# Top-k of query tiles 5 to 7 spread over attention, and attention in two passes over the heads

## Chip, cores and metric

The kernel runs on one core of a Trainium2 chip. The metric is device time in microseconds (us) of one execution; smaller is better. A core has five engines with a queue each, worked off in order: PE (TensorE, matrix products), DVE (VectorE), ACT (ScalarE), POOL (GpSimd) and SP (SyncE, which here only issues DMAs). PE writes into PSUM, and DVE and ACT evict from there into SBUF.

## What is computed

One layer of a streaming encoder, for 1024 new frames (query tiles 0 to 7 of 128 rows) and 32 frames of a running stream with 512 cached ones (tile 8). Sizes: D_MODEL 1024, 8 query heads on 4 key/value heads of 64, 8 indexer heads, 8 recurrent heads, hidden layer 4096.

```python
xn = rms_norm(x, norm_mix)
zq, zk, zv, ziq, zik, ziw, zs = split(xn @ w_in)
# group A: sparse attention
dots  = einsum('bthd,bsd->bths', qi, ki_all) * IDX_DIM ** -0.5
score = einsum('bths,bth->bts', relu(dots), wi)          # indexer
score = where(arange(L) < (qpos // 64 + 1) * 64, score, -inf)
_, idx = top_k(score, 256 or L // 4)
o_att = softmax attention of q over the chosen keys only
# group B: rwkv7, a matrix state carried along the frames
S = S * w_t - (S kk_t) b_t + v_t k_t ;  y_t = S r_t      # per head
h = x + concat(o_att, o_rwkv) @ w_out
y = h + square(relu(rms_norm(h, norm_ffn) @ w_ff1)) @ w_ff2
```

A query keeps its 256 best keys; for tiles 0 and 1 all admissible keys are kept, so the top-k runs for tiles 2 to 8. The kernel does not gather. It finds each row's threshold and adds a large negative mask to the attention scores of all other keys.

## The kernel before

A framework orders the instructions: each has a priority from its place in the traced program (and from high_priority blocks), and each engine's queue is filled with what is ready in a modelled timeline, by that priority. A tile of memory is given to the next user when all readers of the previous one are done. Generators in the program interleave the stages.

**Input projections** (phase_a). Keys and indexer keys of all tiles, then indexer queries and the scores S.sc[t] of tiles 2 to 8 (idx_tile), then K and Q of attention (norm_tile, 18 calls) and the recurrence's inputs (zs_block, 14 calls, whose matmuls are L440 and whose evictions on ACT are L449 and L450). Scores of tiles 4 to 8 lie in one tile G of 4096 columns, those of 2 and 3 in tiles named AR.

**Top-k** (topk, two generators in tk). The threshold is found bit by bit in 31 rounds. The first group, tiles 2, 3, 4 and 8, counts on DVE (L342); the second, tiles 5, 6 and 7, counts on ACT with the Sign function (L362), three operations and three accumulator reads a round. Three small DVE operations (L364, L365, L367) then set the next threshold, on which the next round waits. step(1) stands behind each norm_tile and each zs_block and takes one step of both generators; step(100) takes what is left of 32. masks() drains the rest: for the second group an exact correction (L342, L381, L382), then for both Sign, Square, a running count and the mask (L396, L397, L402, L403, L404). It works in S.eq, which is the tile KB of the pool te, and in junk tiles named AR.

**Recurrence** (rwkv_all). Five units of 256 frames (the last one of 32). Per unit: a front (lora products, decay sums L647, KB and AR by L681, products L712 masked by L715 into G, four transposes L824, a triangular inverse on POOL in L829 and L831, transposes L835 and L840), a join (L768 to L779), token transposes (L746 to L752) and four sequential steps per unit (L876 to L911), then a norm. Units 0, 2 and 4 use tiles KB, AR and G of the pool rp. Units 1 and 3 use KB of te and AR and G of S.tk, the very tiles of the top-k. The triangular inverse has one set of buffers for all units.

**Attention** (attn_all). Items are pairs of key/value head j and tile t, for j = 0 to 3 and t in ORD. At t = 8 and t = 0 prep transposes the head's keys (L1062, L1064, L1067, L1068) into K and Kl, which have one buffer. Per item: query (L1080 to L1087), scores for two heads (L1099, L1100, masked and reduced by L1102 on DVE, exponential L1105 on ACT, into one of three tiles s), then turn (transposes L1123, copies L1124 alternately on ACT and DVE) and product (L1139 with V, L1143 to L1146, stored by L1147). The next item's begin runs between the turns of the present one.

The program calls the recurrence eight steps ahead, then masks(), and then takes one step of ga (attention) and one of gr (recurrence) in turn. Output projection (project, L1256; tiles 0 to 2 by project_early, into tiles G, KB and AR of rp) and the MLP (L1320, L1340) follow.

Of the kernel before, what the change touches and what calls it, by code (L numbers as in the profile page):

```python
# [53 lines left out]
F32 = mybir.dt.float32  # L54
F32R = mybir.dt.float32r
BF16 = mybir.dt.bfloat16
# [10 lines left out]
NT = 9  # L67
# [83 lines left out]
def phase_a(S, pwx, pwy, pa, pi, px, xp, ps, late):  # L151
    nc, I, O = S.nc, S.I, S.O
# [73 lines left out]
    iw = pa.tile([128, NT, 8], F32, name="iw")  # L226

    G = S.tk.tile([128, 4096], F32, name="G")
    S.sc, c = {}, 0
    for t in range(4, NT):  # L230
        n = 664 if t == 8 else 128 * (t + 1)
        S.sc[t] = G[:, c:c + n]
        c += n
    for t in (2, 3):
        S.sc[t] = S.tk.tile([128, 128 * (t + 1)], F32, name="AR", bufs=4)
# [1 line left out]
    for SL in SLS:  # L237
        X = K()
# [4 lines left out]
        X.off = S.tk.tile([128, 2, len(SL)], F32, name="off" + str(len(SL)))  # L243
    ones = S.tk.tile([128, 1], F32, name="ones")
    nc.gpsimd.memset(ones, 1.0)
    junk, junk2 = [S.tk.tile([128, 1024], BF16, name="AR", bufs=4) for _ in range(2)]

    kiA = pi.tile([128, 1024], F32R, name="kiA")
    kiB = pi.tile([128, 1024], F32R, name="kiB")
# [95 lines left out]
    def topk(X):  # L345
# [9 lines left out]
        for i in range(30, -1, -1):  # L355
            if X.exact:
                count(X, ALU.is_lt, c_of, S.sc)
            else:
                for j, t in enumerate(X.SL):
                    r = rows_of(t)  # L360
                    n = S.sc[t].shape[1]
# [11 lines left out]
        if not X.exact:  # L373

            count(X, ALU.is_gt, c_of, S.sc)
            for j, t in enumerate(X.SL):
                r = rows_of(t)
                n = S.sc[t].shape[1]
                s = S.sc[t][:r, :n]
                e = S.eq[j % 2][:r, :n]  # L380
                nc.vector.tensor_scalar(e, s, c_of(j, r), BIG, op0=ALU.is_le, op1=ALU.mult)  # L381
                nc.vector.tensor_tensor_reduce(out=e, in0=e, in1=s, op0=ALU.add, op1=ALU.min, scale=1.0, scalar=FMAX,  # L382
                                               accum_out=cns[:r, j:j + 1])
                yield
            nc.vector.tensor_scalar(need, cnt, 256.0, None, op0=ALU.is_ge)
            nc.vector.tensor_tensor(cns, cns, cf, op=ALU.subtract)
            nc.vector.tensor_tensor(cns, cns, need, op=ALU.mult)
            nc.vector.tensor_tensor(cf, cns, cf, op=ALU.add)

        nc.vector.tensor_scalar(cns, cf, -1.0, None, op0=ALU.mult)  # L390
        for j, t in enumerate(X.SL):
            r = rows_of(t)
            g = S.sc[t][:r]
            a = [x[:r, j:j + 1] for x in (cnt, cns, need)]
            cum = S.eq[j % 2][:r, :g.shape[1]]
            nc.scalar.activation(g, g, AF.Sign, bias=a[1], accum_out=a[0])  # L396
            nc.scalar.activation(cum, g, AF.Square, accum_out=a[2])  # L397
            nc.vector.tensor_tensor(a[2], a[2], a[0], op=ALU.add)
            nc.vector.tensor_scalar(a[2], a[2], -0.5, 256.0, op0=ALU.mult, op1=ALU.add)
            n = keys_of(t)  # L400
            g, cum = g[:, :n], cum[:, :n]
            nc.vector.tensor_tensor_scan(cum, ones[:r].to_broadcast([r, n]), cum, 0.0, op0=ALU.add, op1=ALU.subtract)  # L402
            nc.vector.scalar_tensor_tensor(cum, cum, a[2], g, op0=ALU.is_gt, op1=ALU.is_gt)  # L403
            nc.scalar.activation(S.mb[t], cum, AF.Copy, scale=-BIG)  # L404
            yield
# [49 lines left out]
    tk = [topk(X) for X in TK]  # L455
# [43 lines left out]

    left = [32 - EARLY * (len(IDXO) - EI), 32]  # L500

    def step(n):
        for i, g in enumerate(tk):
            m = min(n, left[i])
            left[i] -= m
            for _ in range(m):
                next(g)
# [43 lines left out]
            yield  # L551

    def masks():
        for g in tk:
            for _ in g:
                pass
    return main, main2, main3, masks


# [484 lines left out]
def attn_all(S, ap, ps):  # L1044


    nc, I, O = S.nc, S.I, S.O
    items = [(j, t) for j in range(4) for t in ORD]
    J, W = {}, {}

    def prep(j, samp):
# [97 lines left out]

    def begin(k):  # L1150
        j, t = items[k]
        if t == 8 or t == 0:
            prep(j, t == 8)
        query(k)
        yield
        for h in range(2):
            scores(k, h)
            yield
        inverse_sums(k)
        yield  # L1160

    N = len(items)
    for _ in begin(0):
        yield
# [212 lines left out]
MA = 8  # L1377
# [8 lines left out]
RAT = 1  # L1386
XPB = 3
DINV = ()
ORD = [8,0,1,2,3,4,5,7,6]
ZQB = 3  # L1390
ACB = 2
HIM = 2
# [6 lines left out]
SLS = ((2,3,4,8),(5,6,7))  # L1399
IDXO = (2,3,4,5,8,6,7)  # L1400
PH = 4
AHEAD = 6
# [8 lines left out]
def body(tc, I, O, dbg=None):  # L1411
    nc = tc.nc
    S = K()
    S.nc, S.tc, S.I, S.O, S.dbg = nc, tc, I, O, dbg or {}
    pool = lambda **kw: tc.tile_pool(bufs=1, **kw)
    with pool(name="const") as cp, pool(name="dram", space=DRAM) as dp:
# [6 lines left out]
        def opened(name, side="left"):  # L1423
            p = pool(name=name, side=side)
            return p, p.__enter__()
# [5 lines left out]
        mp = S.mp  # L1431
        S.mb = {t: mp.tile([rows_of(t), keys_of(t)], BF16, name=f"mb{t}") for t in range(NT) if t != 7}
        S.xs = mp.tile([128, 8, 64], F32R, name="mb7")
        p1a, S.tk = opened("p1a", "right")
        with pool(name="xnt") as xp, pool(name="psA", space=PSUM) as ps:
            late = {}
# [3 lines left out]
            with pool(name="pi", side="right") as pi:  # L1440
                with pool(name="px", side="right") as px:
                    m1, m2, m3, masks = phase_a(S, pwx, pwy, pa, pi, px, xp, ps, late)
                    g = m1()
# [19 lines left out]
            with pool(name="pq") as pq:  # L1463
                g = m3(pq, 4, 7)
# [3 lines left out]
                gr = rwkv_all(S, RORD)  # L1468
# [17 lines left out]
        ga = attn_all(S, S.at, ps)  # L1486
        for _ in range(ATT0):
            next(ga)
        for i in range(EARLYF, max(AHEAD, MA)):
            if i == MA:  # L1490
                masks()
            next(gr)
        if MA >= AHEAD:
            masks()
        S.G.append(S.tk.tile([128, 2, 4, 4, 128], F32, name="G"))
        raw = wo = None
        gens = [ga, gr]
        while gens or wo is None:
            for g in list(gens):
                with (tc.high_priority(OFF) if g is gr else nullcontext()):  # L1500
# [37 lines left out]
```

## Time and profile before

| what | value |
|---|---|
| median of 3 timed runs | 1797.65 us (1793.79 to 1798.66) |
| profiled execution | 1798.12 us |
| its span, first to last instruction | 1796.3 us |
| mean granted clock of TensorE | 0.927 |
| busy in the span: PE, DVE, ACT, POOL | 93%, 52%, 39%, 34% |

The page gives busy time per engine, busy shares in 40 slices of 45 us (a digit is tenths, 9 is 90% or more), the chain of work that ended last, and the costliest groups of instructions by line. PEclk is the granted clock of TensorE, 1.00 being 2.4 GHz and 0.50 being 1.2 GHz. Groups read: out<-in, shapes, count | busy us, mean ns | idle time of the engine just before them and what ended it. In a stretch, "busy (x)" is the busy time and the number of records; accumulator reads count as records of their own.

### The profile page before, as it was taken

The numbers are of one execution on the slowest core, as the hardware profiler recorded it, in microseconds if no ns is written. First come the engines' busy times: TensorE is split into PE (matmuls) and PEld (weight loads), VectorE is DVE, ScalarE is ACT, GpSimd is POOL, SyncE is SP. The second block draws the span as 40 slices with busy tenths as digits, with TensorE's granted clock in tenths as the row PEclk, the third lists the DMA queues.
The fourth block names the chain that finished last, engine by engine and source line by source line (L and its number), as shares of the span: only waits on it lengthen the run. The fifth ranks groups of instructions, "written<-read, shape, count | busy, mean of one in ns | idle before, by whom it ended". The sixth has DMA issues, their size and how long they took to land.

```text
span 1796.3 us, 30013 instructions
## 1 busy us (share of the span) xinstructions
PE 1663.9 (93%) x11686; PEld 1509.2 (84%) x11686; DVE 936.1 (52%) x1996; ACT 707.6 (39%) x1549; POOL 618.6 (34%) x919
## 2 busy tenths in 40 slices
PE   7999979986569898999899999999999999999999
PEld 6787779986456777767678799999999999999998
DVE  6477889975878687577562533222222222222224
ACT  6365667897446344344641331222222121212120
POOL 7468863353543443056210021222222222222120
PEclk9999989996559697798899999999999999999999
DMA  7211131323110202140323341111111111111105
GB/s 218 54 36 43 42 88 64 110 68 92 29 27 14 40 24 57 26 101 17 98 76 123 121 125 49 46 48 45 49 37 53 42 53 42 47 44 51 36 16 172
DMA packets 180775, 113.25 MB, mean 63 GB/s; under 512 B 51969, under 2 KB 169817, under 8 KB 180633
## 3 DMA queue, kind: packets, MB, share of 16 engines
q1 hardware_dynamic: 171800, 107.00, 21.4%
q10 hardware_dynamic: 8832, 4.33, 0.9%
q8 instruction: 92, 1.51, 0.4%
q14 instruction: 51, 0.41, 0.1%
HBM read 86.29 MB, written 25.01 MB: 62 GB/s over the span
## 4 chain that ended last, share of the span: by engine, by line
PE 63%; DVE 12%; ACT 5%; POOL 4%; issue 3%; DMA 2%; SPq 0%; DVEq 0%; ACTq 0%; POOLq 0%
PE pd L1320 20%; PE pr L1340 10%; PE pc L1340 5%; PE po L1340 5%; PE pd L1256 3%; PE po L1139 2%; DVE AR L342 2%; ACT AR L362 2%; PE ptr L1123 2%; PE pr L1256 2%; PE acc L440 2%; DVE L L824 1%; PE pr L712 1%; POOL tl L829 1%; POOL Yl L831 1%
## 5 line engine op out<-in xcount | busy, mean ns | idle before, releaser
L1320 PE MATMUL pd<-hh,w1h 128*128 128x352 f32 x768 | 248.6, 324 | 2.2 <-issue 1.4
L1320 PE MATMUL pd<-hh,w1l 128*128 128x352 f32 x768 | 248.2, 323 | 0.7 <-DVE w1l L1187 0.7
L1320 PE MATMUL pd<-hl,w1h 128*128 128x352 f32 x768 | 247.5, 322 | 0.0
L1326 DVE TENSOR_TENSOR h2l<-rl,h2h 128x352 fp32r<-128x352 f32 x96 | 56.9, 592 | 277.3 <-ACT h2h L1325 277.3
L1324 POOL TENSOR_TENSOR rl<-rl 128x352 f32<-128x352 f32 x96 | 85.2, 888 | 215.5 <-ACT rl L1323 215.5
L1186 ACT CAST w2h<-w2r 128x512 fp32r<-128x512 f32 x64 | 39.7, 621 | 293.0 <-PE po L1340 144.8
L1320 PEld LDWEIGHTS pd<-hh,w1h 128*128 128x128 f32 x768 | 144.7, 188 | 2.8 <-issue 1.7
L1320 PEld LDWEIGHTS pd<-hh,w1l 128*128 128x128 f32 x768 | 144.8, 189 | 0.9 <-DVE w1l L1187 0.9
L1320 PEld LDWEIGHTS pd<-hl,w1h 128*128 128x128 f32 x768 | 145.3, 189 | 0.0
L1187 POOL TENSOR_TENSOR w2l<-w2r,w2h 128x512 fp32r<-128x512 f32 x32 | 41.6, 1299 | 299.3 <-ACT w2h L1186 288.8
L1340 PE MATMUL pr<-h2h,w2l 128*128 128x352 f32 x384 | 124.3, 324 | 0.0
L1340 PE MATMUL pr<-h2h,w2h 128*128 128x352 f32 x384 | 124.3, 324 | 0.0
L1340 PE MATMUL pr<-h2l,w2h 128*128 128x352 f32 x384 | 124.1, 323 | 0.0
L362 ACT ACTIVATE AR<-G,cnd 128x768 bf16<-128x768 f32 (+2 forms) x93 | 96.7, 1040 | 42.2 <-DVE cnd L367 36.8
L1323 ACT ACTIVATE rl<-pd 128x352 f32<-128x352 f32 x96 | 44.3, 463 | 143.4 <-PE pd L1320 136.9
L1346 DVE TENSOR_TENSOR ya<-ya,pr 128x352 f32<-128x352 f32 x84 | 43.8, 521 | 101.0 <-PE pr L1340 101.0
L829 POOL TENSOR_TENSOR tl<-L,Yl 128x56 f32<-128x56 f32 (+22 forms) x155 | 65.9, 425 | 60.5 <-DVE L L824 50.0
L1105 ACT ACTIVATE s<-s,m 32x544 f32<-32x544 f32 (+8 forms) x72 | 55.4, 770 | 74.8 <-DVE m L1102 74.6
L1123 PE MATMUL ptr<-ident,s 128*128 128x128 f32 (+2 forms) x328 | 69.4, 321 | 16.2 <-ACT s L1105 11.2
L1325 ACT CAST h2h<-rl 128x352 fp32r<-128x352 f32 x96 | 46.6, 485 | 75.3 <-POOL rl L1324 75.3
L1340 PEld LDWEIGHTS pr<-h2l,w2h 128*128 128x128 f32 x384 | 72.3, 188 | 0.1
L1340 PEld LDWEIGHTS pr<-h2h,w2h 128*128 128x128 f32 x384 | 72.2, 188 | 0.1
(443 smaller groups left out, 4655.1 us busy)
## 6 DMA issues: line engine op xcount, KB each, us to landing
w1r<-in_w_ff_dram SPq DMA_DIRECT2D x32, 512.0 KB, 4.1
w2r<-in_w_ff_dram SPq DMA_DIRECT2D x64, 256.0 KB, 2.9
zsd<-zm SPq DMA_DIRECT2D x12, 528.0 KB, 2.7
wraw<-in_w_in_dram SPq DMA_DIRECT2D x24, 256.0 KB, 2.7
wraw<-in_w_in_dram SPq DMA_DIRECT2D x40, 128.0 KB, 2.2
x<-in_x_prompt_dram SPq DMA_DIRECT2D x8, 512.0 KB, 5.0
hres<-hd ACTq DMA_DIRECT2D x16, 256.0 KB, 3.3
out_dram<-hres SPq DMA_DIRECT2D x16, 256.0 KB, 2.3
```

Source lines behind the costliest of these rows:

```text
L362: nc.scalar.activation(junk2[:r, :n], S.sc[t][:r, :n], AF.Sign, bias=c_of(j, r), scale=-1.0, accum_out=cnt[:r, j:j + 1])
L829: eng.tensor_tensor(t_, L[:, 0:j, j:j + 1].to_broadcast([128, j, w]), Y[:, j:j + 1, m:16].to_broadcast([128, j, w]), op=ALU.mult)
L1105: nc.scalar.activation(s, s, AF.Exp, bias=m[:, i:i + 1], scale=-1.0, accum_out=w.m[:, 6 + h:7 + h])
L1123: nc.tensor.transpose(p[:x, i, h, :r], w.s[h][:, c0 + i * 128:c0 + i * 128 + x], S.ident[:r, :r])
L1256: nc.tensor.matmul(acc[:r], a[:, k], b, start=(i == 0), stop=(i == 23))
L1320: nc.tensor.matmul(acc, a[:, k], m[:, k, o:o + n], start=(i == 0), stop=(i == 23))
L1323: nc.scalar.activation(rl, acc, AF.Relu)
L1324: nc.gpsimd.tensor_tensor(rl, rl, rl, op=ALU.mult)
L1325: nc.scalar.copy(h2h[:, o:o + n], rl)
L1326: nc.vector.tensor_tensor(h2l[:, o:o + n], rl, h2h[:, o:o + n].bitcast(F32), op=ALU.subtract)
L1340: nc.tensor.matmul(acc, a[:, k], m[:, o:o + n], start=(i == 0), stop=(i == 11))
L1346: nc.vector.tensor_tensor(y, y, acc, op=ALU.add)
```

## The change

The second top-k group gets every second step only (LATE), is left out of step(100), and its generator is no longer drained before attention but returned by masks() and put into the list of generators that are stepped in turn with attention and recurrence. Its scores get a tile of their own (S.late, 2688 columns) and its junk a tile of its own, both in the pool of the masks; its exact correction and mask build work in tiles named s of the attention pool (three buffers) instead of S.eq. Attention's items are ordered in two passes: all heads over tiles 8, 0, 1, 2, 3, 4, then all heads over tiles 5, 7, 6; prep is run at the head of each pass too. The scratch memory for dynamic DMA is set to 1024 bytes.

```diff
     G = S.tk.tile([128, 4096], F32, name="G")
-    S.sc, c = {}, 0
-    for t in range(4, NT):
-        n = 664 if t == 8 else 128 * (t + 1)
-        S.sc[t] = G[:, c:c + n]
+    S.sc, c = {4: G[:, 0:640], 8: G[:, 640:1304]}, 0
+    for t in SLS[1]:
+        n = 128 * (t + 1)
+        S.sc[t] = S.late[:, c:c + n]
         c += n
...
-    junk, junk2 = [S.tk.tile([128, 1024], BF16, name="AR", bufs=4) for _ in range(2)]
+    junk, junk2 = S.tk.tile([128, 1024], BF16, name="AR", bufs=4), S.junk2
...
-                e = S.eq[j % 2][:r, :n]
+                e = S.at.tile([128, 1024], F32, name="s", bufs=XPB)[:r, :n]
...
-            cum = S.eq[j % 2][:r, :g.shape[1]]
+            cum = (S.eq[j % 2] if X.exact else S.at.tile([128, 1024], F32, name="s", bufs=XPB))[:r, :g.shape[1]]
...
+    rounds = [0]
+
     def step(n):
+        rounds[0] += 1
         for i, g in enumerate(tk):
-            m = min(n, left[i])
+            m = min(n if i == 0 or n > 1 or rounds[0] % LATE == 0 else 0, left[i])
+            if n > 1 and i == 1:
+                m = 0
             left[i] -= m
...
     def masks():
-        for g in tk:
-            for _ in g:
-                pass
+        for _ in tk[0]:
+            pass
+        return tk[1]
...
-    items = [(j, t) for j in range(4) for t in ORD]
+    items = [(j, t) for s in ORDS for j in range(4) for t in s]
...
-        if t == 8 or t == 0:
+        if t in (8, ORDS[0][1], ORDS[1][0]):
             prep(j, t == 8)
...
-ORD = [8,0,1,2,3,4,5,7,6]
+ORDS = ((8, 0, 1, 2, 3, 4), (5, 7, 6))
+LATE = 2
...
+        S.late = mp.tile([128, sum(128 * (t + 1) for t in SLS[1])], F32, name="late")
+        S.junk2 = mp.tile([128, 1024], BF16, name="junk2")
...
-            if i == MA:
-                masks()
             next(gr)
-        if MA >= AHEAD:
-            masks()
+        gm = masks()
...
-        gens = [ga, gr]
+        gens = [ga, gr, gm]
...
-    nc = bacc.Bacc("TRN2", target_bir_lowering=False, num_devices=1)
+    nc = bacc.Bacc("TRN2", target_bir_lowering=False, num_devices=1, dynamic_dma_scratch_size=1024)
```

## Rows read from the trace of the kernel before

**Rows 1.** Page, busy tenths of PE in 40 slices of the span
```profile
PE   7999979986569898999899999999999999999999
```

**Rows 2.** Stretches: length; busy us (records) of PE, PEld, DVE, ACT, POOL; PEclk; DMA; GB/s
```profile
205.00:260.00 55.00, 42.26 (x208) 35.54 (x208) 52.65 (x132) 33.87 (x69) 37.61 (x48) 0.88 0.27 74
260.00:380.00 120.00, 115.27 (x718) 113.52 (x716) 104.30 (x305) 97.32 (x217) 50.67 (x67) 1.00 0.29 88
...
434.00:540.00 106.00, 67.68 (x431) 54.29 (x430) 79.17 (x180) 52.95 (x117) 47.64 (x78) 0.52 0.19 33
540.00:600.00 60.00, 56.57 (x449) 43.65 (x448) 45.27 (x88) 31.17 (x71) 25.45 (x52) 0.80 0.09 24
600.00:730.00 130.00, 115.50 (x1322) 91.66 (x1322) 94.62 (x219) 56.81 (x146) 47.08 (x102) 0.83 0.18 36
...
1040.00:1796.00 756.00, 749.25 (x4674) 747.00 (x4672) 212.67 (x363) 159.01 (x289) 162.49 (x144) 1.00 0.20 56
```

**Rows 3.** Waits of PE at 205 to 416 us: total, times, longest
```profile
PE acc L440 <- ACT tm L450: 16.8, 10, 7.9
PE acc L440 <- DVE zq L202: 4.4, 1, 4.4
```

**Rows 4.** Timeline of DVE and ACT, 245 to 252 us (start, length, engine, line)
```profile
245.10 3.70 DVE L367 TENSOR_SCALAR cnd<-cnd 128x4 int32<-128x4 int32 x1
...
249.64 0.93 ACT L362 ACTIVATE AR<-G,cnd 128x768 bf16<-128x768 f32 x1 [4.65 <-DVE cnd L367]
...
251.74 0.53 ACT L449 ACTIVATE zm<-acc,mu 128x352 f32<-128x352 f32 x1
```

**Rows 5.** Group of L362 on the page; its records by stretches
```profile
L362 ACT ACTIVATE AR<-G,cnd 128x768 bf16<-128x768 f32 (+2 forms) x93 | 96.7, 1040 | 42.2 <-DVE cnd L367 36.8
...
205.00:260.00 55.00, 20.41 (x36) 0.88 0.27 74
...
416.00:470.00 54.00, 16.97 (x30) 0.53 0.33 72
```

**Rows 6.** Timeline around the recurrence's units 0 and 1
```profile
405.70 0.66 ACT L404 ACTIVATE mb<-KB 32x544 bf16<-32x544 f32 x1
...
467.58 3.02 DVE L669 TENSOR_TENSOR k<-k,tmp 128x1024 f32<-128x1024 f32 x1
...
477.12 1.01 DVE L342 TENSOR_SCALAR_CACHE_REDUCE AR<-G,cnd 128x768 bf16<-128x768 f32 x1
...
506.35 1.06 ACT L404 ACTIVATE mb<-KB 128x1024 bf16<-128x1024 f32 x1 [0.55 <-DVE KB L403]
...
509.98 4.54 DVE L835 STREAM_TRANSPOSE G<-Yl 32x512 f32<-32x512 f32 x4 [3.66 <-POOL Yl L831]
...
516.35 1.22 DVE L681 TENSOR_TENSOR KB<-k,D 64x1024 f32<-64x1024 f32 x1
...
531.39 1.16 ACT L779 COPY G<-pc 32x512 f32<-32x512 f32 x2 [3.52 <-PE pc L776]
...
557.34 3.95 DVE L824 STREAM_TRANSPOSE L<-G 32x1024 f32<-32x1024 f32 x2
...
560.30 0.46 PE L746 MATMUL pr<-ident,KB 64*128 64x64 f32 x4
...
568.28 0.33 PE L876 MATMUL pc<-VU,G 64*64 64x64 f32 x2
```

**Rows 7.** Preparing a head's keys, 434 to 933 us; a load in the chain
```profile
L1064 PE MATMUL ptr<-ident,k 128*128 128x128 f32 x48 | 10.3, 354 | 5.5 <-DVE m L1102 4.5 <-POOL k L1062 1.0
...
L1068 DVE TENSOR_TENSOR Kl<-ptr,K 128x512 fp32r<-128x512 f32 x12 | 8.2, 682 | 3.0 <-ACT K L1067 3.0
...
600.51 2.60 DMA kp<-out_dram
```

**Rows 8.** Threshold operations of DVE at 205 to 260 and 416 to 470 us
```profile
L367 DVE TENSOR_SCALAR cnd<-cnd 128x4 int32<-128x4 int32 x8 | 7.1, 883 | 0.1
...
L367 DVE TENSOR_SCALAR cnd<-cnd 128x3 int32<-128x3 int32 x5 | 0.8, 163 | 0.1
```

## The prediction

> **What bounds the kernel now.** I read the slices of the whole span first [rows 1]: from about 1040 us to the end PE is at 9 in every slice. The row for 1040 to 1796 us [rows 2] says the same, 749 of 756 us busy at a granted clock of 1.00, so nothing before it can shorten that part; an edit pays only by letting it start earlier. Next the table by stages [rows 2]. From 260 to 380 us (input projections, top-k beside them) PE is busy 115.3 of 120 us at clock 1.00: bound by PE. From 434 to 540 us, where attention and the recurrence begin, it is busy only 67.7 of 106 us, and at a clock of 0.52, the lower level of 1.2 GHz nearly throughout; that is about 35 us of full-speed work in 106. DVE has 79.2 of 106 us there. From 540 to 600 and from 600 to 730 us PE is busy 94% and 89%, at 0.80 and 0.83. So the slack lies in 205 to 260 us (42.3 of 55 us, DVE 52.7) and above all in 434 to 600 us.
>
> The waits say what ends last. In the projections PE waited 16.8 us for the second eviction L450 of an accumulator and once 4.4 us for L202 [rows 3]. The longest of the first kind, 7.9 us, can be followed [rows 4]: DVE's L367, an operation on four columns, took 3.70 us, ACT idled 4.65 us at the head of its queue with a top-k count (L362) that needed the threshold behind it, and the evictions L449 and L450 stood behind that count until 251.74. In attention's beginning the queue of DVE holds the rest of the top-k: the last counts, minima and scans of tiles 5 to 7, from L342 at 477.12 to the last mask L404 at 506.35 [rows 6], and what the top-k reads and writes lies in memory that the second unit of the recurrence (unit 1) needs. That unit's rows [rows 6] are the core of my argument, below.
>
> **The change part by part.** The sum is made against the profiled execution, 1798.1 us, which is 0.5 above the median of the three timed ones.
>
> *Half rate.* The program has 32 calls of step; the second group made 32 steps there and now makes 16, so 16 of its 31 rounds come later in program order. What is queued is decided by readiness as well: the trace has 30 L362 records (counts and accumulator reads, 5 rounds) after 416 us [rows 5], though all stood earlier in the program, and 6 rounds (36 records) by 260 us where the program had asked for 18. So rounds were late against the program and hence ahead of the evictions in rank; at half rate they rank behind. I take 10 rounds after 416 us instead of 5. Gain in the projections: at most the waits of [rows 3], 16.8 + 4.4, some 21 us; at least nothing, for no instruction is added there. Nearest is the 7.9 us case [rows 4], which is of this very kind, while the first group's counts on DVE stay. I take **-8**.
>
> *Rounds and masks beside attention.* A round is three counts and their reads on ACT, 16.97/5 = 3.4 us [rows 5]. Five more rounds are 17 us (none to 11 rounds: 0 to 37 us) on an ACT that is busy 53.0 of 106 us in this stretch [rows 2]. Behind a waiting L362 stand attention's exponentials L1105 and the copies L1086 and L1124, for which PE waits; over the whole kernel ACT idled 36.8 us before L362 for a threshold [rows 5], 1.2 us per round. Ten rounds would lose 12 us, five did lose 6. The mask build (DVE and ACT, as long as before) only moves. It now borrows one of attention's three s buffers six times, where it had a buffer of its own: the next item's scores may wait, 0 to (507 - 477)/6 = 5 us each, mostly under PE work on the current item. Together between 0 and 37 + 30 = +67; I take **+6**, the waits of five more rounds.
>
> *Scores in space of their own.* Unit 1's keys are ready when L669 ends, at 467.58 + 3.02 = 470.6 us; its KB waits for the buffer in which the masks are built. The last mask is copied out at 506.35 + 1.06 = 507.4 us, and KB is written at 516.35, behind L835 in DVE's queue [rows 6]. G, where the scores lie, and an AR tile used as junk are free no sooner than the last counts. After the change all three come free with the first group, whose last mask was done at 405.70 + 0.66 = 406.4 us [rows 6]. Then unit 1's products (L712), which come after KB (516.35) and before L824 (557.34), need not stand in PE's queue in front of unit 0's token transposes (L746, from 560.30) and its first step (L876, 568.28), although unit 0's join was copied out at 531.39 + 1.16 = 532.6 (L779). Unit 0's steps could start up to 568.3 - 532.6 = 36 us sooner. Unit 1's transposes L824 (557.34) could follow unit 0's L835 (509.98 + 4.54 = 514.5) at once, 43 us sooner. The units run one after another to the end of attention's stage, so what unit 0 gains the chain gains, as long as PE has room: between 434 and 600 us it has [rows 2]. Bounds 0 and -43. Not all of it will come, since DVE, with 79 of 106 us, takes this work earlier while it also has attention and the masks, and attention keeps its own pace. I take **-25**.
>
> *Second pass.* Items and their sizes stay; the heads' small tiles now follow one another, and the large ones come last. prep is run four times more: 8 transposes each, 32 x 10.3/48 us = 6.9 us on PE [rows 7], which is near its limit there, so on the path. The ACT and POOL copies, the DVE subtractions (8 x 0.68 us [rows 7]) and the K load hide under the transposes and products of the large item before. V does not hide: its only buffer is free after the last product of the head before, and the first product of tile 5 follows shortly. A load of such a size took 2.60 us [rows 7]; with four to eight transposes of 0.215 us over it 0.9 to 1.7 us are left, and I take the upper end, since a store may stand ahead of it in SP's queue: four times 1.7, 7 us. Bounds 7 (V hidden) and 7 + 4 x 2.6 + 2.8 = 20 (V bare, and half of the 5.5 us that the eight preps of before waited at L1064 [rows 7]); **+14**. The loads join SP's queue with the q loads and the output stores, without anything slow in it.
>
> *Other edits.* The smaller scratch for dynamic DMA costs nothing: every DMA is issued from SP or ACT. Shifting the two work tiles and the scores' memory changes no instruction. The projection of tiles 0 to 4 could now begin earlier, but its buffers wait for the last unit's G as before: 0.
>
> Sum: -8 + 6 - 25 + 14 = -13, so 1785 us.
>
> **A rule of the Trainium skill against it.** While POOL was busy 37.6 of 55 us (205 to 260 us [rows 2]), the four-column L367 took 0.883 us on average, and 0.163 us in the quieter stretch from 416 to 470 us [rows 8]. The moved rounds come beside POOL's triangular inverse, most of POOL's 47.6 us at 434 to 540 us. The Trainium skill, "SBUF — State Buffer", section "Who interferes with whom", says that a VectorE operation with two SBUF inputs, or in a two-port mode, and a GpSimd operation lock each other out for the whole instruction; by that rule the moved rounds would be slowed, which is rival (c); the rows agree in direction.
>
> **The rivals.**
> (a) *Slower: lock-step of ACT and DVE in attention.* Attention, not the recurrence, sets the pace, and each late round puts two handovers (DVE to ACT and back) into queues on which PE waits. If all 16 rounds come late, each with 1.2 us of ACT waiting and one count (3.4/3 = 1.1 us) ahead of a needed operation: 16 x 2.3 = 37 us, less the 12 that five such rounds cost already, +25. With half the gain of the recurrence (-12) and -8, +14: +19, 1817 us. It decides from the point where the rounds run beside attention's exponentials at more than half of ACT's time. For it: DVE and ACT wait for each other already [rows 5]; against: ACT has half its time free in that stretch. Chance 0.28.
> (b) *A draw.* The recurrence is held by unit 0's own inverse and gains only 10, the rest as above: -8 + 6 - 10 + 14 = +2, 1800 us. Chance 0.12.
> (c) *DVE slowed beside POOL.* The moved rounds' threshold operations take what [rows 8] show for a busy POOL: three at up to 0.883 instead of 0.163 us, 2.2 us a round, 22 us for ten rounds, of which some 17 fall on the path where DVE is fullest: 1785 + 17 = 1802 us, 0.06.
> (d) *The change does not do what it says.* Rounds are placed by readiness, so they run where they ran; projections gain nothing, the late rounds cost nothing, but the memory is free: -25 + 14 with less of the first (-17) is -3, 1795 us. For it: five rounds lie after 416 us though the program puts all before [rows 5], so its order is only one of two hands. 0.06.
> (e) *More.* Unit 1's work fills the idle PE at 434 to 540 us, and the clock, granted at 0.52 there, rises: -43 for the recurrence, -15 for the projections, +14 + 4: -40, 1758 us. For it: only 35 us of full-speed work in 106. Chance 0.17.
> Forecast (1770 to 1792): 0.31.
>
> **How the numbers follow.** The likeliest case is the forecast, 1785 us. Changes under 0.3% (5.4 us) can hardly be told from none: 1792.3 to 1803.0 counts as the same. Faster: forecast and (e) with a part of (d), 0.50; same: 0.21, (b), (c) and the rest of (d); slower: (a) and the edge of (c), 0.29. Eight times in ten the time lies between 1755 (most of case e) and 1826 (case a, and a quarter of the way from it to the sum with both costs at their upper bounds, -8 + 67 - 25 + 20 = +54); the forecast's own range is 1770 to 1792.
>
> **What the profile after would show.** Half rate: about 60 L362 records after 416 us instead of 30, and less waiting of PE for L450. Memory: unit 1's KB before 500 us, its L712 before unit 0's L746, its L824 near 515 to 530 us, and a PE share above 0.75 in 434 to 540 us. Second pass: 48 + 32 L1064 transposes of full size, and PE waits at L1139 for V. The stage 1040 to 1796 us must keep its 756 us and only start earlier, by 13 us. Wrong would be: KB of unit 1 still after 510 us (no gain), waits of L1105 or L1124 behind L362 above 20 us (case a), or L364, L365 and L367 at around a microsecond beside POOL (case c).

## Result and profile after

The changed kernel took **1813.8 us** (median of 4 runs, 1813.5 to 1817.5) against 1795.9 us of the kernel before on the same chip: 1.0103 times, 95% interval [1.0082, 1.0125], so 18.5 us slower. The forecast was 1785 us and faster. The time lies near that of rival (a), 1817 us, but what it named is not what happened.

The profiled execution has a span of 1812.1 us. Its stretches, in the columns of [rows 2]:

```profile
205.00:260.00 55.00, 40.94 (x201) 33.89 (x200) 51.52 (x128) 34.27 (x68) 39.89 (x49) 0.88 0.26 72
260.00:380.00 120.00, 114.90 (x706) 113.24 (x704) 105.94 (x301) 95.51 (x212) 47.11 (x63) 0.98 0.29 88
434.00:540.00 106.00, 81.55 (x478) 65.72 (x478) 82.04 (x176) 55.48 (x124) 50.16 (x91) 0.50 0.22 43
540.00:600.00 60.00, 41.00 (x369) 32.74 (x371) 42.90 (x92) 25.73 (x59) 37.41 (x59) 0.63 0.18 29
600.00:730.00 130.00, 119.61 (x1511) 94.89 (x1508) 93.00 (x218) 63.13 (x171) 44.85 (x88) 0.87 0.19 45
...
1056.00:1812.00 756.00, 748.77 (x4671) 746.52 (x4670) 212.72 (x363) 159.22 (x289) 161.96 (x144) 1.00 0.20 56
```

The last 756 us are as long as before and only start 16 us later. The projections have not gained. From 434 to 540 us PE is busier (77% against 64%), but at 1.2 GHz throughout, and from 540 to 600 us, where it had been 94% busy at a clock of 0.80, it is 68% busy at 0.63.

PE's waits at 205 to 416 us, against [rows 3]; then DVE and ACT at 247 to 254 us, against [rows 4]:

```profile
PE acc L440 <- ACT tm L450: 16.7, 7, 8.0
PE acc L440 <- DVE zq L202: 4.4, 1, 4.4
PE acc L440 <- POOL wlx L173: 3.5, 2, 3.2
```

```profile
247.34 3.70 DVE L367 TENSOR_SCALAR cnd<-cnd 128x4 int32<-128x4 int32 x1
...
251.88 0.93 ACT L362 ACTIVATE junk<-late,cnd 128x768 bf16<-128x768 f32 x1 [4.67 <-DVE cnd L367]
...
253.98 0.53 ACT L449 ACTIVATE zm<-acc,mu 128x352 f32<-128x352 f32 x1
```

The same 3.70 us operation, the same count at the head of ACT's queue, the same 8 us of PE: half rate left the case it was priced by untouched, and one wait, for the weight split L173 on POOL, is new. The counts L362 on the page and in two stretches, against [rows 5]:

```profile
L362 ACT ACTIVATE junk<-late,cnd 128x768 bf16<-128x768 f32 (+2 forms) x93 | 96.8, 1041 | 44.3 <-DVE cnd L367 33.5
```

```profile
205.00:260.00 55.00, 20.40 (x36) 0.88 0.26 72
416.00:470.00 54.00, 20.37 (x36) 0.61 0.33 70
```

Six rounds run by 260 us, exactly as before, and 36 records (40 up to 480 us) after 416 us instead of 30. Beginnings of attention and recurrence, against [rows 6] (lines from about 502 on stand 5 lower: L686 is the old L681, L829 L824, L751 L746, L881 L876):

```profile
479.43 2.43 DVE L686 TENSOR_TENSOR KB<-k,D 64x1024 f32<-64x1024 f32 x2
...
525.81 0.69 PE L751 MATMUL pr<-ident,KB 64*128 64x64 f32 x4 [0.34 <-ACT tmp L117]
...
525.91 3.88 DVE L829 STREAM_TRANSPOSE L<-G 32x1024 f32<-32x1024 f32 x2
...
542.04 1.12 PE L881 MATMUL pc<-VU,G 64*64 64x64 f32 x16 [0.91 <-ACT G L784]
...
543.10 0.84 ACT L404 ACTIVATE mb<-s 128x768 bf16<-128x768 f32 x1
...
559.54 1.06 ACT L404 ACTIVATE mb<-s 128x1024 bf16<-128x1024 f32 x1 [5.94 <-DVE s L403]
```

The memory did what was forecast: unit 1's KB is written at 479 us instead of 516, and unit 0's first step runs at 542 instead of 568. The units' norms are stored at 667.5 to 927.5 us instead of 684.5 to 933.7. But attention's last store (L1152, the old L1147) leaves at 961.8 us instead of 931.6, so attention and no longer the recurrence ends last; and when project_early (L1261) is done, PE stands still. SP's queue and PE there:

```profile
961.84 0.32 SPq L1152 DMA_DIRECT2D od<-t  x1
...
972.17 0.32 SPq L1266 DMA_DIRECT2D hd<-KB  x1
975.10 0.33 SPq L1237 DMA_DIRECT2D xr<-in_x_prompt_dram  x1
975.47 0.98 SPq L1245 DMA_DIRECT2D of<-od  x2
...
980.65 0.80 PE L1261 MATMUL pd<-G,o 128*128 128x512 f32 x1 [9.23 <-ACT o L1247]
```

In the kernel before, these loads (xr, of) were issued at 933 and 934 us, under project_early's matmuls:

```profile
925.57 6.36 SPq L1147 DMA_DIRECT2D od<-t  x2
933.29 0.34 SPq L1232 DMA_DIRECT2D xr<-in_x_prompt_dram  x1
```

The products with V and the keys' transposes, 434 to 975 us (group, busy us and mean ns, idle of PE before them), the latter against [rows 7]:

```profile
L1144 PE MATMUL po<-ph,vp 128*64 128x128 f32 x576 | 57.2, 311 | 3.6 <-DVE t L1151 2.4 <-DVE ph L1129 1.0 <-ACT ph L1129 0.2
...
L1069 PE MATMUL ptr<-ident,k 128*128 128x128 f32 (+1 forms) x84 | 15.9, 314 | 9.3 <-DVE Kl L1073 9.1 <-ACT ph L1129 0.2
```

PE never waited for V. It waited 9.1 us for the copies of K.

### The profile page after: what moved, and what is told of

Its sections match the earlier page's. It is cut to its first block, busy times and chain, and to the rows that moved or that the text cites. A ratio compares the mean times of both kernels' runs of the same rounds, so it can differ in the third digit from the quotient of the medians.

```text
span 1812.1 us, 30125 instructions
## 1 busy us (share of the span) xinstructions
PE 1669.5 (92%) x11718; PEld 1514.6 (84%) x11718; DVE 945.6 (52%) x2004; ACT 714.7 (39%) x1557; POOL 631.4 (35%) x927
## 4 chain that ended last, share of the span: by engine, by line
PE 63%; DVE 14%; ACT 5%; POOL 3%; issue 2%; DMA 1%; SPq 0%; DVEq 0%; ACTq 0%; POOLq 0%
PE pd L1325 20%; PE pr L1345 10%; PE pc L1345 5%; PE po L1345 5%; PE pd L1261 3%; DVE AR L342 3%; PE po L1144 2%; ACT junk L362 2%; PE ptr L1128 2%; PE pr L1261 2%; DVE L L829 2%; PE pr L717 2%; PE acc L440 1%; PE pd L1104 1%; POOL Yl L836 1%
## 5 line engine op out<-in xcount | busy, mean ns | idle before, releaser
L362 ACT ACTIVATE junk<-late,cnd 128x768 bf16<-128x768 f32 (+2 forms) x93 | 96.8, 1041 | 44.3 <-DVE cnd L367 33.5
L1328 ACT ACTIVATE rl<-pd 128x352 f32<-128x352 f32 x96 | 44.3, 463 | 144.4 <-PE pd L1325 139.2
L836 POOL TENSOR_TENSOR Yl<-Yl,tl 128x56 f32<-128x56 f32 (+22 forms) x155 | 72.7, 469 | 11.2
```

The lines of the kernel that those rows point to most:

```text
L362: nc.scalar.activation(junk2[:r, :n], S.sc[t][:r, :n], AF.Sign, bias=c_of(j, r), scale=-1.0, accum_out=cnt[:r, j:j + 1])
L836: eng.tensor_tensor(Y[:, 0:j, m:16], Y[:, 0:j, m:16], t_, op=ALU.add)
```

## Experiments

All were run with the kernel before beside them; microseconds are worked out as ratio x 1796. The intervals reach 0.1 to 0.26% to each side (2 to 5 us), that of own_tile_tk 0.34%. The runs of two_own_tk, full_own_tk and own_tile_tk scatter over 12 to 17 us, those of each other kernel over 10 at most.

| kernel | passes | second top-k group | mask build in | pool of the scores | ratio [95%] | us against before |
|---|---|---|---|---|---|---|
| scores_own_tk | 1 | full rate, drained | KB of te | S.tk | 0.9996 [0.9985, 1.0008] | -1 |
| mem_own_tk | 1 | full rate, drained | own tile | S.tk | 0.9903 [0.9877, 0.9928] | -17 |
| mem_own_off | 1 | full rate, drained | own tile | S.tk | 0.9925 [0.9904, 0.9946] | -13 |
| mem_own_rat | 1 | full rate, drained | own tile | S.tk | 0.9929 [0.9907, 0.9950] | -13 |
| half_own_tk | 1 | half rate, drained | own tile | S.tk | 0.9955 [0.9938, 0.9971] | -8 |
| prep_own_tk | 1, keys twice | full rate, drained | own tile | S.tk | 0.9998 [0.9985, 1.0011] | 0 |
| mem_s_tk | 1 | full rate, drained | s tiles | S.tk | 1.0082 [1.0065, 1.0098] | +15 |
| mem_only | 1 | full rate, drained | s tiles | masks | 1.0113 [1.0095, 1.0132] | +20 |
| two_rat | 2 | full rate, drained | own tile | S.tk | 0.9972 [0.9961, 0.9984] | -5 |
| two_own_tk | 2 | full rate, drained | own tile | S.tk | 1.0000 [0.9979, 1.0022] | 0 |
| two_pass | 2 | full rate, drained | s tiles | masks | 1.0170 [1.0146, 1.0194] | +31 |
| full_own_tk | 2 | full rate, masks beside | own tile | S.tk | 1.0010 [0.9994, 1.0026] | +2 |
| full_rate | 2 | full rate, masks beside | s tiles | masks | 1.0098 [1.0077, 1.0118] | +18 |
| own_tile_tk | 2 | half rate, beside | own tile | S.tk | 1.0050 [1.0016, 1.0084] | +9 |
| late_tk | 2 | half rate, beside | s tiles | S.tk | 1.0034 [1.0019, 1.0048] | +6 |
| tail_act | 2 | half rate, beside | s tiles | masks | 1.0092 [1.0077, 1.0107] | +17 |
| the change | 2 | half rate, beside | s tiles | masks | 1.0103 [1.0082, 1.0125] | +18.5 |

**One part at a time.** After reading the changed profile I held that the recurrence, now early, takes the place of attention's first items. mem_only puts back the rate, the draining and the single pass:

```diff
-        gm = masks()
+        for _ in masks():
+            pass
...
-        gens = [ga, gr, gm]
+        gens = [ga, gr]
...
-    items = [(j, t) for s in ORDS for j in range(4) for t in s]
+    items = [(j, t) for j in range(4) for t in ORD]
```

> The kernel before with one part of the change alone: the scores of tiles 5 to 7 and the second junk tile in space of their own, the mask build in attention's s tiles. The second top-k group keeps its full rate, is drained ahead of attention as before, and attention keeps its single pass. Theory of the prediction (memory): unit 1's KB is no longer bound to the last mask, the recurrence sets the end, 25 us gained, about 1773 us. Rival (attention sets the end): the recurrence is earlier, its norms by some 10 us, but attention's last store is where it was (931 us) and the time stays within 1788 to 1802 us.

1815.5 us: the whole loss, without second pass or late rounds. But it carries two things of the change that are not the recurrence's memory: masks built in attention's s tiles, and a gap of PE near 975 us as in the change.

two_pass adds the second pass to it; full_rate is the change with LATE = 1.

> The same as mem_only and the second pass over the heads for tiles 5, 7 and 6; the top-k is still at full rate and drained ahead of attention, so that only half rate and the stepping beside attention are missing from the whole change. Theory of the prediction: +14 us against mem_only (7 of transposes, 7 of loads of V). If only the transposes count: +7. If the second pass is what made the changed kernel slow: within 5 us of its 1814. If the late rounds and masks did it: below 1803.

> The changed kernel with LATE = 1: all 31 rounds of the second group are asked for beside the projections, and only its correction and mask build are left for the list that is stepped with attention. If late rounds are what stalls attention's beginning (rival a of the prediction): 12 to 25 us faster than the change, 1790 to 1802. If it is the masks of DVE work, three s buffers and the earlier recurrence: the same as the change within 5 us, last mask still after 530 us.

1825.4 us and 1814.6 us. The second pass cost 10 us more, and the rate alone moved nothing that could be told here: 1.0098 at full rate, 1.0103 at half. Against two_pass, stepping the masks beside attention took 13 us off. Both kernels carry a gap of PE of 7.6 us before the output projection, so the parts had to be told apart on a cleaner base.

**The gap of PE before the output projection.** tail_act moves only three stores from SP's queue to ACT's:

```diff
-    nc.sync.dma_start(S.hd[t * 128:t * 128 + r], x)
+    (nc.scalar if tag == "pr" else nc.sync).dma_start(S.hd[t * 128:t * 128 + r], x)
```

> The changed kernel with one edit: project_early's three result stores go into ACT's DMA queue instead of SP's. In the changed kernel PE idles 9.2 us at 971 to 980 us; SP's queue stood 11.4 us with a store hd<-KB that waited for project_early's last tile, and the loads of<-od of the next projection stood behind it. If that order of the queue makes the gap: the loads leave at about 966 us instead of 975, the gap shrinks to 0 to 3 us and the time falls by 6 to 12 us, with the clock that falls there (0.85 in 965 to 1000 us) up too. If the gap is due to the tiles' memory being given free only by that store: no change, 1814.

1812.0 us, and the gap is the same (9.0 us):

```profile
972.53 0.33 ACTq L1266 DMA_DIRECT2D hd<-KB  x1
975.46 0.33 SPq L1237 DMA_DIRECT2D xr<-in_x_prompt_dram  x1
```

With nothing of the store in SP's queue the load of xr still left 2.9 us behind that store. In the change the chain of work that ended last has the store's transfer there:

```profile
972.17 2.65 DMA hd<-KB
```

The theory of the queue fell; that the load waits for memory, given free when the store has landed, is what late_tk puts to the test. late_tk moves the memory and nothing else:

```diff
-        S.late = mp.tile([128, sum(128 * (t + 1) for t in SLS[1])], F32, name="late")
-        S.junk2 = mp.tile([128, 1024], BF16, name="junk2")
         p1a, S.tk = opened("p1a", "right")
+        S.late = S.tk.tile([128, sum(128 * (t + 1) for t in SLS[1])], F32, name="late")
+        S.junk2 = S.tk.tile([128, 1024], BF16, name="junk2")
```

> The changed kernel with S.late and the second junk tile taken out of the pool of the masks and put into S.tk, on the other side of the memory; no instruction is added or removed. In the changed kernel these 12.8 KB lie under the pool rp and push it up, so that the first o2 tile of the output projection comes to lie over rp's VU, rh and st, where before all its tiles lay over attention's alone; its loads were then behind project_early's last store (972 us). If this memory makes the gap of 9.2 us at 971 to 980 us: no gap of PE over 2 us after 950 us, 1800 to 1806 us. If the gap has another cause, or PE has nothing to do there anyway: 1811 to 1816 us.

1802.8 us, and SP's queue in late_tk reads:

```profile
960.99 0.33 SPq L1237 DMA_DIRECT2D xr<-in_x_prompt_dram  x1
961.37 0.99 SPq L1245 DMA_DIRECT2D of<-od  x2
...
971.86 0.33 SPq L1266 DMA_DIRECT2D hd<-KB  x1
```

The loads leave 14 us earlier, ahead of project_early's last store, and PE has no wait of a microsecond from 945 to 985 us. That last store leaves at 971.9 us in late_tk and 972.2 in the change, but the last 756 us of the span begin at 1043.4 and 1056.1: the difference arises behind it. So the place of 12.8 KB in each partition costs 0.69%, 12 us.

**Where the masks are built.** own_tile_tk is late_tk with a work tile of its own:

```diff
-        S.junk2 = S.tk.tile([128, 1024], BF16, name="junk2")
+        S.wk2 = S.tk.tile([128, 1024], F32, name="junk2")
+        S.junk2 = S.wk2.bitcast(BF16)[:, :1024]
...
-                e = S.at.tile([128, 1024], F32, name="s", bufs=XPB)[:r, :n]
+                e = S.wk2[:r, :n]
```

> late_tk, and the exact correction and mask build of tiles 5 to 7 in one work tile of their own instead of attention's three s tiles (all else as in the change: half rate, masks beside attention, two passes). If the borrowed s tiles hold attention back at 540 to 570 us: attention's sixth store falls before 560 us instead of after 572, and 5 to 15 us are gained against late_tk. If DVE's queue (mask work and the earlier recurrence) does it: the same as late_tk within 4 us.

1.0050 against 1.0034: no gain; the intervals overlap, and the medians (1808.6 and 1802.8 us) lie 6 us apart the other way. Attention's sixth store leaves at 586.1 us instead of 594.1, but its last one at 968.7 instead of 959.4. Beside attention, no cost of borrowing the s tiles can be told. But own_tile_tk has a gap that late_tk has not, and it could hide a gain of that size: with the memory in S.tk, but attention's last store at 968.7 us and project_early's last product at 969.2, PE again stands still, for 7.8 us. mem_own_tk is mem_only with own tile and S.tk; mem_s_tk takes the own tile away again; scores_own_tk builds in KB, as the kernel before.

> The kernel before with memory alone changed: scores of tiles 5 to 7 and one work tile for their mask build in S.tk; full rate, masks drained ahead of attention, a single pass. mem_only was 20 us slower than before, with the mask build in attention's s tiles and with the gap of PE at the end. If these two made it slow: 1785 to 1797 us. If the recurrence's second unit, free from the masks, takes the place of attention's first items on PE and DVE: unit 0's first step (L876 of before) still near 536 us, fewer than five stores of attention by 547 us, 1800 to 1808 us.

> mem_own_tk (1780 us) with one thing put back: correction and mask build of the second group in attention's three s tiles, as in the change (drained ahead of attention, a single pass). mem_only is the same with the 12.8 KB under rp: 1815 us, of which the memory's place should be 11 (the change against late_tk). So 1804 if the rest, 24 us, is the s tiles: attention's first stores then fall behind the first two masks (after 520 us, in mem_own_tk from 481). If the s tiles do not hold attention: 1780 to 1785 us, and the place of the memory is worth all.

> The same as mem_own_tk, but the masks are built in S.eq as in the kernel before, so that unit 1's KB still waits for the last mask and only its G and AR are free early. If it is KB that starts the early recurrence: the order and the time of before, 1790 to 1799 us, unit 0's first step near 568 us. If G and AR are enough: as mem_own_tk.

1780.1 (below both ranges expected), 1810.2 (above its 1804) and 1796.5 us. My theory of the early recurrence fell with the first: attention's first three stores leave 1 to 8 us later than before (479.5, 485.4 and 500.0 us there), but its last one leaves 18 us earlier, and 17 us are gained. The stretch 480 to 520 us (columns of [rows 2]) and attention's first stores in mem_own_tk, L1149 being its L1147:

```profile
480.00:520.00 40.00, 36.50 (x178) 29.57 (x179) 30.72 (x80) 22.22 (x58) 24.23 (x49) 0.56 0.09 25
```

```profile
480.75 0.35 SPq L1149 DMA_DIRECT2D od<-t  x1
...
493.47 0.32 SPq L1149 DMA_DIRECT2D od<-t  x1
...
507.51 0.38 SPq L1149 DMA_DIRECT2D od<-t  x1
```

The same stretch and ACT's first masks and exponentials of attention in mem_s_tk:

```profile
480.00:520.00 40.00, 19.98 (x89) 17.39 (x89) 33.61 (x65) 14.76 (x28) 29.89 (x49) 0.50 0.06 15
```

```profile
506.82 0.84 ACT L404 ACTIVATE mb<-s 128x768 bf16<-128x768 f32 x1 [3.53 <-DVE s L403]
...
518.99 0.95 ACT L404 ACTIVATE mb<-s 128x896 bf16<-128x896 f32 x1 [11.33 <-DVE s L403]
...
523.47 1.06 ACT L404 ACTIVATE mb<-s 128x1024 bf16<-128x1024 f32 x1 [1.12 <-DVE s L403]
...
529.66 0.74 ACT L1107 ACTIVATE s<-s,m 32x544 f32<-32x544 f32 x1
```

Drained ahead of attention, the masks hold all three s tiles, and attention's first exponential runs after the last mask (in mem_own_tk it runs at 452.2 us). This is 32 us, most of what made mem_only slow. In the change the masks come behind attention's first items, and nothing of this size is seen. In scores_own_tk unit 1's KB is written at 517.9 us, as before, and the time is as before too: G and AR set free bring nothing by themselves, KB must be free as well. (scores_own_tk has the small scratch for dynamic DMA too, which so cost nothing.)

mem_own_off and mem_own_rat ask how far this gain hangs on the order of the queues: OFF = -230 instead of -200, and two steps of attention at every third turn.

> mem_own_tk (1780 us) with the recurrence's offset of priority at -230 instead of -200, which moves the recurrence a little back against attention and shuffles the queues; nothing is added or removed. It measures how far the time moves with the order of the queues alone. If the gain of the memory is a mechanism: 1776 to 1786 us. If it was a lucky order: 1788 to 1800.

> mem_own_tk (1780 us) with attention at two steps at every third turn. There attention and the recurrence end together (both at 913 us). If the balance of the two is what counts, then attention now ends well before the recurrence, whose end moves back, and the time is 1783 to 1795 us; if attention is simply too slow everywhere: 1772 to 1779 us.

1781.4 us both: the first in the range of a mechanism, the second between its two ranges. A shuffle of the queues moved the time by 1 us (medians) to 4 us (ratios), with intervals overlapping; more steps for attention brought nothing in the single pass.

**The second pass.** two_own_tk is mem_own_tk with the two passes; prep_own_tk has the single pass, but prepares the keys twice, as the two passes need it:

```diff
-        if t == 8 or t == 0:
+        if t in (8, 0, 5):
```

> mem_own_tk (1780 us) and the second pass over the heads for tiles 5, 7 and 6; the second group is still at full rate and drained ahead of attention. Prediction's term: +14 us, 1794. If only the 32 transposes count: +7, 1787. If the second pass is what keeps the change from the gain of the memory, because attention's large items then come last and end after the recurrence: attention's last store 25 us or more after the recurrence's last norm (in mem_own_tk both at 913 us), +18 to +28, 1798 to 1808 us. If the late rounds and masks do it: at most 1790.

> mem_own_tk (1780 us; a single pass) with the second preparation of each head's keys put in, ahead of tile 5, where the single pass has no need of it: the 32 transposes, copies, subtractions and four loads of K and V of the second pass, without its order of the items. two_own_tk, with the order too, took 16.5 us more than mem_own_tk. If the preparation is the price, as the prediction had it (+14): 1792 to 1797 us. If the order of the items is (large ones last, attention ending after the recurrence): the 7 us of transposes at most, 1780 to 1788 us.

1796.6 and 1795.0 us: each 0.95 to 0.97%, 17 us, above mem_own_tk. In a single pass the preparation alone costs all of the 17 us. It does not follow that the order of the items, which I had come to suspect, costs nothing: in two_own_tk attention's last store leaves at 959.2 us, after project_early's last (948.4), and PE stands still behind it; prep_own_tk has no such gap. PE in two_own_tk:

```profile
967.52 0.79 PE L1258 MATMUL pd<-G,o 128*128 128x512 f32 x1 [9.29 <-DMA gbc<-in_norms_dram]
```

How the 17 us of the two passes are made up is open. Group and waits of PE at 434 to 975 us, first the group in mem_own_tk, then group and waits in prep_own_tk (L1066 is the old L1064, L1125 the old L1123):

```profile
L1066 PE MATMUL ptr<-ident,k 128*128 128x128 f32 (+1 forms) x52 | 10.1, 316 | 5.4 <-DVE m L1104 4.5 <-POOL k L1064 1.0
```

```profile
L1066 PE MATMUL ptr<-ident,k 128*128 128x128 f32 (+1 forms) x84 | 18.3, 344 | 8.0 <-DVE Kl L1070 6.7 <-POOL k L1064 1.3
```

```profile
PE ptr L1066 <- DVE Kl L1070: 6.7, 2, 4.4
...
PE ptr L1125 <- DVE Kl L1070: 4.1, 2, 3.9
```

8.2 us more of transposes, and 10.8 us in which PE waits for Kl, the last of the chain transpose, copy K on ACT, difference Kl on DVE (1.3 us in mem_own_tk). The whole stage agrees: from 425 us to the last 756 us of the span PE is busy 529.9 us against 519.6 and idle 84.4 against 75.8. two_rat gives attention more steps in the two-pass order:

```diff
         while gens or wo is None:
+            turn += 1
             for g in list(gens):
...
-                    for _ in range(RAT if g is ga else 1):
+                    for _ in range(2 if g is ga and turn % 3 == 0 else 1):
```

> two_own_tk (1796.6 us) with one edit: attention takes two steps instead of one at every third turn of the list. In two_own_tk the recurrence's last norm stood at 899 us and attention's last store at 959 us, with 8 us of idle PE behind 933. If the second pass costs what it does because attention falls behind the recurrence: attention's end moves forward by 15 us or more, the norm back, and 4 to 12 us come back, 1785 to 1793 us. If the extra preparation is the cost: 1794 to 1800 us.

1789.2 us, 0.28% (5 us) better than two_own_tk. There the last norm stood at 899 and attention's last store at 959 us; now they stand at 925 and 939, and the gap is gone. So some of the second pass's cost can be had back by balance; the intervals touch, so the 5 us are likely rather than shown.

**Masks beside attention, and the rate.** full_own_tk has the masks beside attention at full rate, half_own_tk the half rate in the single pass:

> two_own_tk, but the correction and mask build of the second group are not drained ahead of attention: they are stepped beside it, as in the change; rounds at full rate. It differs from own_tile_tk (1808.6) by the half rate alone and from two_own_tk by the place of the masks alone. If masks beside attention cost nothing once they have a tile of their own: as two_own_tk within 5 us. Prediction's term for late rounds and masks: +6 between full_own_tk and own_tile_tk, less the 8 of the projections; so the same within 5 us.

> mem_own_tk (1780 us) with the half rate alone: the second group takes one step at every second call beside the projections, the rest is drained ahead of attention; a single pass. Prediction's terms: -8 in the projections, +6 for late rounds, so 1778. If the modelled timeline places the rounds anyhow and the projections do not gain: the projections' last store within 2 us of mem_own_tk's or later, and the later rounds delay the masks: 1782 to 1795 us.

full_own_tk is as two_own_tk (+2 us, not to be told from 0): with a tile of their own, masks beside attention cost nothing that can be told. Half rate is not in the single pass: +0.52% (9 us) from mem_own_tk to half_own_tk, intervals apart. From full_own_tk to own_tile_tk it is +0.40% (7 us), with intervals that overlap, and from full_rate to the change +0.05%. PE's waits at 205 to 425 us in half_own_tk; mem_own_tk has 16.0 us in the first line, and the one of L173 not at all:

```profile
PE acc L440 <- ACT tm L450: 18.0, 8, 8.2
...
PE acc L440 <- POOL wlx L173: 3.5, 2, 3.2
```

The projections' last store leaves at 434.6 us instead of 428.2 (in the change 436.0 instead of 429.9).

## Why the prediction was wrong, step by step

By one chain of runs, each with one edit more, the change is made up so: memory -17, second pass +17, masks beside attention +2, half rate +7, s tiles -3 (for each of these three the intervals overlap), place of the new memory +12: together +18. The parts do not simply add: on other bases the second pass measured +10 (two_pass against mem_only), half rate +1 (the change against full_rate) and the place +6 (mem_only against mem_s_tk). The gap of PE before the output projection is why in part: it is in two_own_tk, full_own_tk and own_tile_tk (7.8 to 9.8 us), not in late_tk, and again in the change, so the +17 of the second pass holds one and the +12 of the place brings it back.

**Scores in space of their own** (forecast -25, measured -17). Right in mechanism: KB before 500 us, L829 within 515 to 530 us, PE above 0.75 in 434 to 540 us, all as forecast; but it is the masks' leaving KB that it takes, as the scores' own space by itself brought nothing (scores_own_tk). The size was off by 8 us: in mem_own_tk unit 0's first step comes 24 us earlier (544.0 against 568.3) and the last norm 20 us (913.8 against 933.7), and attention's end now binds too (913.3). In the change the last norm keeps only 6.

**Second pass** (forecast +14, measured +17). The 6.9 us of transposes were 8.2. The other half was priced as loads of V, for which PE never waited. In prep_own_tk and in the change it is the chain of K's copies, which I had declared hidden under the large item before: the right sum came in part by luck.

**Half rate** (forecast -8, measured +9 in the single pass, +7 and +1 in two). This step failed. I read the trace rightly, that readiness and not the program order places the rounds, and still took a gain from the program order. Ten rounds after 416 us were assumed; there are under seven. The eviction waits stayed at 16.7 us. What changed is POOL's order near 390 us: in the change POOL does the recurrence's L674 (392.3 us) ahead of the weight split L173 (394.7 us), for which PE waits 3.2 us; before, L173 came first (384.7 and 387.4 us, and L669, the change's L674, at 391.5):

```profile
392.33 2.37 POOL L674 TENSOR_TENSOR k<-k,tmp 128x1024 f32<-128x1024 f32 x1 [1.77 <-ACT tmp L673]
394.65 3.11 POOL L173 TENSOR_TENSOR wlx<-wraw,whx 128x224 fp32r<-128x224 f32 x2
```

```profile
387.37 0.85 POOL L173 TENSOR_TENSOR wlx<-wraw,whx 128x224 fp32r<-128x224 f32 x1 [1.91 <-ACT whx L172]
...
391.45 2.39 POOL L669 TENSOR_TENSOR k<-k,tmp 128x1024 f32<-128x1024 f32 x1 [2.60 <-ACT tmp L668]
```

At full rate (full_rate, full_own_tk) L173 stays first and the projections' last store leaves at 430.1 and 431.2 us, so the rate turned them round; why the planner does so was not tried. The 6 us lost in the projections are shown. In the single pass the whole kernel is 9 us slower with them; in the change, against full_rate, nothing of them is left at the end, and why is open. For this edit rival (d), that it does not do what it says, was true of the order of the rounds.

**Rounds and masks beside attention** (forecast +6). Free within 2 us, as far as masks in a tile of their own go. L362's waits for L367 fell from 36.8 to 33.5 us (all idle time before L362 rose from 42.2 to 44.3), and after 416 us there was one, of 8.4 us, so the lock-step of rival (a) was not there. Rival (c) did not come either: the late rounds' L367 took 0.151 to 0.170 us. Its price was misread as well: 0.883 us is a mean with single operations of 0.17 to 3.70 us in it, and of the first group's four columns; the second group's, of three columns, took 0.299 us there. The late rounds ended at 472 us, and POOL was busy only 5.3 of 36 us from 434 to 470 us, so they do not test what the Trainium skill, "SBUF — State Buffer", section "Who interferes with whom", says of VectorE beside a GpSimd operation.

**"Shifting ... changes no instruction", priced at 0** (measured +12). This is the second step that failed, and the larger one. Two sentences put it at nothing: that shifting the scores' memory changes no instruction, and that the projection's buffers wait as before. The first is true and beside the point. By the program's allocation (no view shows addresses), S.late (2688 columns of 4 bytes) and the junk tile (1024 of 2) lie in the first pool on the left, under rp and attention's pool, so these move up by 12.8 KB in each partition; the output projection's tiles, which before lay over attention's memory only, then reach down into rp, which project_early holds to its end. So the loads wait for project_early's last store to land, and PE has nothing left to do under them. What the place would cost where attention ends early no run shows: in each kernel with the scores in the masks' pool its last store leaves at 962 us or later. And a late end of attention is enough by itself for such a gap: own_tile_tk, two_own_tk and full_own_tk have it with the memory in S.tk, where attention ends with project_early or after it, so that its products no longer cover the loads.

With the half rate at +9 (masks included) for -2 and the place of the memory at +12 for 0, the sum of the prediction turns from -13 to about +10; the smaller gain of the memory (+8) and the dearer second pass (+3), less the 3 us of the s tiles, make the rest of +18. This is the one chain of runs above; on the change's own base half rate is +1.

**What beats both kernels** is the memory alone: mem_own_tk, with the scores and one work tile in S.tk, at 1780.1 us, 0.9903 [0.9877, 0.9928] of the kernel before.

## What to carry to other kernels

A tile that is given space of its own also takes it from under others: before pricing such an edit at zero, list which later pools lie over which earlier ones, before and after, and who holds those to the end. Where a planner places work by readiness, changing how often the program asks for it need not move that work (here 36 records by 260 us at either rate), so look in the trace whether the order is the program's at all. When a change bundles several edits, price and run them one by one, and on more than one base, since their costs need not add: here a gain of 17 us was in the bundle and was spent twice over.

## What was not expected of the hardware

From 434 to 540 us PE was 77% busy in the change, against 64% before, and yet was granted 0.50 (1.2 GHz) throughout, 0.52 before; from 540 to 600 us, with 68% instead of 94%, 0.63 instead of 0.80. More work in that first stretch did not bring the higher clock by itself: from 434 to 540 us mem_own_rat and two_rat, 74% busy, were granted 0.58, the change at 77% 0.50. No run varied this alone, so what would have is open.
